# Three steps by seven block products, placed late, in the attention groups of a two-layer decoder trunk

## The chip, the cores and the metric

The kernel runs on one core of a Trainium2 chip. The metric is the device time of one execution in microseconds (us); the times named are medians of three runs. Lower is better. Engine names are those of the profile: PE is the matrix engine, PEld its weight loads, DVE the vector engine, ACT the scalar engine, SP the engine whose queue issues the weight transfers.

## The reference

A two-layer decoder trunk on a sequence of 256 tokens, width 2048, all in float32. Layer 0 mixes tokens by causal trailing means, layer 1 by differential attention; each is followed by a SwiGLU block. The change concerns layer 1:

```python
hn = rmsnorm(h, norm_mix[1])
qkv = hn @ w_qkv                       # 2048 x 6144: q, k, v
s = q k^T / sqrt(128) + ALiBi bias, causal;  p = softmax(s), for each of 8 heads twice
a = p[:, :, 0] - lam * p[:, :, 1]
o = rmsnorm(a @ v) * subln_g * (1 - lambda_init)
h = h + o @ w_o                        # 2048 x 2048
h = h + (silu(hn2 @ wg) * (hn2 @ wu)) @ wd     # 5632 wide, both layers
```

## The kernel before, in words

Every large product is made in **groups**. A group is the 256-token activation times 1024 columns of weights, summed over the whole contraction of 2048 in eight **steps** of 256 each. A step takes one transfer of 1 MB from the SP queue (`raw`, three buffers, L109): four blocks B12, B11, B22, B21 of 128 x 512 weights. Float32 accuracy comes from splitting each operand into a high half and a low half: ACT casts `raw` to `whi` (L115), DVE subtracts to get `wlo` (L116); these two have three buffers each. Each block product is then three PE matmuls of 512 columns: high by high, high by low, low by high (L178 to L180).

A **plain** step has eight block products, 24 matmuls, into PSUM banks 4 to 7. A step **by seven** uses a Strassen-Winograd form: seven block products, 21 matmuls, of which some take sums of blocks. For these DVE makes the sums `tsum` (L121, L123, L124; one buffer), ACT their high half `thi` (L130), DVE their low half `tlo` (L131). Only three of the four raw blocks have to be split then (`whi`, `wlo` of 1536 columns in place of 2048). Its products go to all eight banks; banks 0 to 3 are used by no plain step. When a group ends, `combined` (L195) adds the banks up.

Banks 0 to 3 also serve as scratch (`aux`) for everything between the groups: transposes, attention scores, the products with v. So a step by seven cannot begin before the scratch work that was put into the group's early steps has let go of these banks.

The activations are prepared once: `pair` (L245) transposes 256 of the contraction and splits it, for a step by seven with eight slots (four blocks and four sums of them), otherwise with four. `products` (L163) can run a plain step from either layout.

The groups in layer 1 are: four for q and k (L574; each followed by two attention heads, `head` L544, whose work falls into the next group's early steps), two for v (L593; each followed by four heads' output work), two for the output projection (L612). Then come the groups of the SwiGLU block. The lists `SEVEN...` name the step numbers done by seven: 2, 4 and 6 in the SwiGLU groups, 4 and 6 in those of attention, in the order 0 to 7.

The tiles `tsum`, `thi`, `tlo` and the four sums `c` lie in the pool of the stage: `qk_sums` while q and k are made, `out` for v and the output. Pool `attn_tmp` holds a head's working tiles. The order of each engine's instructions is set at compile time by a list scheduler from the program's order and a model of readiness; each engine then runs its own list in order, and semaphores make it wait.

## Time and profile before

| | before |
|---|---|
| median of 3 runs (lowest to highest) | 1843.76 us (1843.35 to 1843.92) |
| profiled execution, its own time | 1843.5 us |
| its span, first to last instruction | 1841.7 us |
| mean granted PE clock | 0.999 |
| PE busy | 1825.5 us, 8201 matmuls |
| DVE busy | 1615.7 us |
| ACT busy | 1043.0 us |
| HBM traffic | 353.36 MB read, 193 GB/s |
| transfers of 1 MB for q and k, v, output | 32, 16, 16 |

Busy times are unions of an engine's instructions. A matmul's duration in the profile is longer than the distance from one to the next, because they are pipelined; the distance is read from start times. A wait is put down to the engine that released it.

### The profile page before, as it was taken

What the parts mean: (1) busy time and instruction counts of PE and PEld (TensorE: products, weight loads), DVE (VectorE), ACT (ScalarE), POOL (GpSimd) and SP (SyncE); (2) the same over time, 40 slices, a digit from 0 to 9 for tenths busy, and PEclk for the clock granted to TensorE, in tenths of its full rate; (3) what the DMA queues carried; (4) which work ended last, traced back from release to release, by engine and by line L of the source; (5) the groups of instructions that cost most, each with busy time, mean ns of one, the idle gap of its engine ahead of it and who ended that gap; (6) DMA issues with size and microseconds to landing.
All of it is one profiled execution on the core that took longest, in us unless ns stands there. A gap on an engine that the chain in (4) does not pass through costs nothing.

```text
span 1841.7 us, 20907 instructions
## 1 busy us (share of the span) xinstructions
PE 1825.5 (99%) x8201; PEld 1493.0 (81%) x8201; DVE 1615.7 (88%) x1676; ACT 1043.0 (57%) x1010; POOL 0.7 (0%) x6
## 2 busy tenths in 40 slices
PE   9999999999999999999999999999999999999998
PEld 6788888888888888888888888788888888888886
DVE  6989998898989899988878779998989899998986
ACT  6655545556554556665566666555555555545553
POOL 0000000000000000000000000000000000000000
PEclk9999999999999999999999999999999999999999
DMA  7555555555555555554554454555555555565552
GB/s 274 183 205 183 198 210 192 211 195 196 202 197 204 201 188 183 206 183 168 176 175 169 168 183 175 209 201 187 204 203 206 191 197 186 207 225 206 202 189 112
DMA packets 50642, 356.80 MB, mean 194 GB/s; under 512 B 6000, under 2 KB 6128, under 8 KB 8048
## 3 DMA queue, kind: packets, MB, share of 16 engines
q1 hardware_dynamic: 49824, 353.85, 54.5%
q10 hardware_dynamic: 720, 1.62, 0.2%
q8 instruction: 64, 1.05, 0.2%
q14 instruction: 34, 0.28, 0.0%
HBM read 353.36 MB, written 2.10 MB: 193 GB/s over the span
## 4 chain that ended last, share of the span: by engine, by line
PE 95%; DVE 2%; ACT 1%; issue 1%; DMA 1%; SPq 0%; DVEq 0%; ACTq 0%
PE b L180 90%; PE b L250 2%; DVE wlo L116 1%; PE b L554 1%; PE b L345 1%; DMA x_tok<-x_n 1%; PE b L584 0%; PE b L342 0%; DMA raw<-w_gu 0%; DVE tlo L131 0%; ACT whi L115 0%; PE b L600 0%; DVE tsum L121 0%; PE b L598 0%; PE b L599 0%
## 5 line engine op out<-in xcount | busy, mean ns | idle before, releaser
L115 ACT CAST whi<-raw 128x1536 fp32r<-128x1536 f32 (+1 forms) x330 | 583.9, 1770 | 572.7 <-PE b L180 486.6
L180 PE MATMUL b<-whi,xp 128*128 128x512 f32 x2814 | 905.9, 392 | 0.8 <-DVE c L203 0.7
L116 DVE TENSOR_TENSOR wlo<-raw,whi 128x1536 fp32r<-128x1536 f32 (+1 forms) x330 | 695.5, 2108 | 178.8 <-ACT whi L115 178.6
L180 PEld LDWEIGHTS b<-whi,xp 128*128 128x128 f32 x2814 | 526.3, 188 | 109.7 <-DVE c L203 1.1
L180 PE MATMUL b<-wlo,xp 128*128 128x512 f32 x1407 | 550.0, 391 | 1.7 <-DVE wlo L116 1.7
L180 PE MATMUL b<-whi,h 128*128 128x512 f32 x1108 | 354.5, 390 | 0.0
L180 PEld LDWEIGHTS b<-wlo,xp 128*128 128x128 f32 x1407 | 264.3, 188 | 55.2 <-DVE wlo L116 1.9
L131 DVE TENSOR_TENSOR tlo<-tsum,thi 128x2048 fp32r<-128x2048 f32 x111 | 253.6, 2284 | 8.0 <-ACT thi L130 8.0
L180 PEld LDWEIGHTS b<-whi,h 128*128 128x128 f32 x1108 | 207.4, 188 | 43.2
L130 ACT CAST thi<-tsum 128x2048 fp32r<-128x2048 f32 x111 | 211.9, 1909 | 16.7 <-DVE tsum L124 16.6
L180 PE MATMUL b<-wlo,h 128*128 128x512 f32 x554 | 215.8, 390 | 0.0
L180 PE MATMUL b<-thi,xp 128*128 128x512 f32 x616 | 214.7, 390 | 0.0
L121 DVE TENSOR_TENSOR tsum<-raw 128x1024 f32<-128x1024 f32 x111 | 135.4, 1220 | 2.1 <-DMA raw<-w_v 0.5
L180 PEld LDWEIGHTS b<-thi,xp 128*128 128x128 f32 x616 | 115.4, 188 | 24.4 <-ACT thi L130 0.9
L180 PEld LDWEIGHTS b<-wlo,h 128*128 128x128 f32 x554 | 104.0, 188 | 21.3
L180 PE MATMUL b<-tlo,xp 128*128 128x512 f32 x308 | 121.1, 393 | 0.0
L180 PE MATMUL b<-thi,h 128*128 128x512 f32 x240 | 83.7, 389 | 0.0
L124 DVE TENSOR_TENSOR tsum<-tsum,raw 128x512 f32<-128x512 f32 x111 | 76.4, 688 | 2.2
L123 DVE TENSOR_TENSOR tsum<-tsum,raw 128x512 f32<-128x512 f32 x111 | 76.0, 684 | 0.7
L180 PEld LDWEIGHTS b<-tlo,xp 128*128 128x128 f32 x308 | 57.8, 188 | 16.3 <-DVE tlo L131 4.5
L180 PE MATMUL b<-whi,oT 128*128 128x512 f32 x216 | 69.1, 393 | 0.0
L180 PEld LDWEIGHTS b<-thi,h 128*128 128x128 f32 x240 | 45.1, 188 | 9.2
(147 smaller groups left out, 1196.4 us busy)
## 6 DMA issues: line engine op xcount, KB each, us to landing
raw<-w_gu SPq DMA_DIRECT2D x176, 1024.0 KB, 4.8
raw<-w_down SPq DMA_DIRECT2D x88, 1024.0 KB, 4.8
raw<-w_qk SPq DMA_DIRECT2D x32, 1024.0 KB, 4.8
raw<-w_v SPq DMA_DIRECT2D x16, 1024.0 KB, 4.9
raw<-w_o SPq DMA_DIRECT2D x16, 1024.0 KB, 4.8
raw<-pool_w SPq DMA_DIRECT2D x2, 1024.0 KB, 14.0
x_tok<-x_n SPq DMA_DIRECT2D x2, 768.0 KB, 8.8
w<-pool_w SPq DMA_DIRECT2D x2, 512.0 KB, 6.3
```

Of the source, the lines that this page charges most:

```text
L115: nc.scalar.copy(hi[:, lo_block:], raw[:, lo_block:])
L116: nc.vector.tensor_tensor(lo[:, lo_block:], raw[:, lo_block:], f32(hi[:, lo_block:]), ALU.subtract)
L121: nc.vector.tensor_tensor(t[:, T1:T3 + 1], raw[:, B11:B22 + 1], raw[:, B12:B12 + 1].broadcast_to([P, 2, 512]), ALU.add)
L123: nc.vector.tensor_tensor(t[:, T2], t[:, T1], raw[:, B22], ALU.add)
L124: nc.vector.tensor_tensor(t[:, T4], t[:, T2], raw[:, B21], ALU.add)
L130: nc.scalar.copy(hi, t)
L131: nc.vector.tensor_tensor(lo, t, f32(hi), ALU.subtract)
L180: nc.tensor.matmul(ps[b], x, y[:, block], start=first, stop=(left[b] == 0))
L250: nc.tensor.transpose(ps[:, i, 1 - t if seven else t], src(i, t), ident)
L345: nc.tensor.matmul(yp[g][t], u, v[:, at], start=(at == 0 and j == 0), stop=(at == 3 and j == 2))
L554: nc.tensor.matmul(sc[:, :nk], qk[:, 0, c, qb * P:(qb + 1) * P], qk[:, 1, c, :nk], start=True, stop=True)
```

## The change

Step 2 joins the steps by seven in the four groups of q and k, the two of v and the first of the output; the second output group keeps 4 and 6. In the seven changed groups the steps run in the order 0, 1, 3, 5, 4, 2, 6, 7, so that the three by seven stand fifth, sixth and seventh. `thi` and `tlo` get two buffers there. To make room in SBUF, the head's `bias` tile goes from two buffers to one and `qk` from three to two. The activation tiles of step 2 (`xp2`, `oT2`) are prepared with eight slots.

```diff
-SEVEN_QKV = (4, 6)
-SEVEN_O = (4, 6)
+SEVEN_QKV = (2, 4, 6)
+SEVEN_O = (2, 4, 6)
+
+LATE = (0, 1, 3, 5, 4, 2, 6, 7)
...
-    def sum_halves(pool, t):
-        hi = pool.tile([P, 4, 512], F32R, name="thi")
-        lo = pool.tile([P, 4, 512], F32R, name="tlo")
+    def sum_halves(pool, t, bufs):
+        hi = pool.tile([P, 4, 512], F32R, name="thi", bufs=bufs)
+        lo = pool.tile([P, 4, 512], F32R, name="tlo", bufs=bufs)
...
-    def group(steps, pool, by_bank=0):
+    def group(steps, pool, by_bank=0, bufs=1):
...
-                w.append(sum_halves(pool, t))
+                w.append(sum_halves(pool, t, bufs))
...
-            bias = at.tile([P, 2 * P], F32, name="bias")
+            bias = at.tile([P, 2 * P], F32, name="bias", bufs=1)
...
-            cs = combined(group([(xp[p], p in SEVEN_QKV, w_qk[g, p]) for p in range(NP)], hq), hq)
+            cs = combined(group([(xp[p], p in SEVEN_QKV, w_qk[g, p]) for p in LATE], hq, bufs=2), hq)
...
-                qk = at.tile([P, 2, 2, S], F32, name="qk", bufs=3)
+                qk = at.tile([P, 2, 2, S], F32, name="qk")
...
-            cs = scaled(combined(group([(xp[p], p in SEVEN_QKV, w_v[g, p]) for p in range(NP)], op_), op_), (r_col, r_col))
+            cs = scaled(combined(group([(xp[p], p in SEVEN_QKV, w_v[g, p]) for p in LATE], op_, bufs=2), op_), (r_col, r_col))
...
-        for g in range(2):
-            cs = combined(group([(oT[p], p in SEVEN_O, w_o[g, p]) for p in range(NP)], op_), op_)
+        for g, (by_seven, order) in enumerate(((SEVEN_O, LATE), (SEVEN_O[1:], range(NP)))):
+            cs = combined(group([(oT[p], p in by_seven, w_o[g, p]) for p in order], op_, bufs=2), op_)
```

## The prediction

> **What bounds the kernel now.** I read the page's first part, then the grouped instructions by shape, the windows, the waits, and the timeline of single groups.

> ```profile
> span 1841.7 us, 20907 instructions
> PE 1825.5 (99%) x8201; PEld 1493.0 (81%) x8201; DVE 1615.7 (88%) x1676; ACT 1043.0 (57%) x1010; POOL 0.7 (0%) x6
> ```
> ```profile
> core 0: us, PE busy (x) PEld busy (x) DVE busy (x) ACT busy (x) POOL busy (x), PEclk, DMA share, GB/s
> 853.70:901.50 47.80, 47.80 (x226) 38.92 (x225) 38.94 (x62) 28.89 (x42) 0.00 (x0) 1.00 0.51 176
> 239.00:282.00 43.00, 43.00 (x191) 35.63 (x190) 39.06 (x34) 21.52 (x14) 0.00 (x0) 1.00 0.58 213
> 820.20:835.70 15.50, 15.50 (x70) 12.83 (x69) 8.48 (x5) 8.28 (x7) 0.00 (x0) 1.00 0.58 204
> ```
> ```profile
> PE b L180 <- DVE wlo L116: 1.7, 1, 1.7
> PE b L325 <- DVE xt L328: 2.0, 2, 1.7
> ```

> The windows are one period of the q and k groups with its two heads, a stretch of the SwiGLU block, and the second half of a q and k group. PE is busy in all of each; DVE has idle time, 8.86 us of 47.8 in the q and k period (47.80 - 38.94). The last two rows head PE's list of waits in the whole span: 1.7 and 2.0 us in all. So PE bounds, and what PE doesn't have to do comes off the time as long as DVE and ACT still feed it. DVE is the next engine, at 88%.

> How far apart are matmuls? A plain step of the first q and k group:

> ```profile
> 778.51 0.61 PE L180 MATMUL b<-whi,xp 128*128 128x512 f32 x2
> ...
> 783.95 0.61 PE L180 MATMUL b<-whi,xp 128*128 128x512 f32 x2
> ```

> The pattern (two, then one with `wlo`) repeats eight times between these two starts: 24 matmuls in 5.44 us, 0.2267 us each. A plain step costs PE 24 x 0.2267 = 5.44 us, one by seven 21 x 0.2267 = 4.76 us.

> **The change part by part.** *PE.* Seven groups lose three matmuls each: 21 x 0.2267 = **-4.76 us**. Nothing is added: `pair` makes four transposes in either layout, `combined` is needed already, and the banks are the same. Four plain steps still stand ahead of the first step by seven, so the scratch banks are asked back as late as now. [...]

> *DVE and ACT.*

> ```profile
> L116 DVE TENSOR_TENSOR wlo<-raw,whi 128x2048 fp32r<-128x2048 f32 x219 | 501.1, 2289 | 162.8 <-ACT whi L115 162.8
> L131 DVE TENSOR_TENSOR tlo<-tsum,thi 128x2048 fp32r<-128x2048 f32 x111 | 253.6, 2284 | 8.0 <-ACT thi L130 8.0
> L130 ACT CAST thi<-tsum 128x2048 fp32r<-128x2048 f32 x111 | 211.9, 1909 | 16.7 <-DVE tsum L124 16.6
> L116 DVE TENSOR_TENSOR wlo<-raw,whi 128x1536 fp32r<-128x1536 f32 x111 | 194.4, 1752 | 16.0 <-ACT whi L115 15.7
> L121 DVE TENSOR_TENSOR tsum<-raw 128x1024 f32<-128x1024 f32 x111 | 135.4, 1220 | 2.1 <-DMA raw<-w_v 0.5
> L124 DVE TENSOR_TENSOR tsum<-tsum,raw 128x512 f32<-128x512 f32 x111 | 76.4, 688 | 2.2
> L123 DVE TENSOR_TENSOR tsum<-tsum,raw 128x512 f32<-128x512 f32 x111 | 76.0, 684 | 0.7
> L268 DVE TENSOR_TENSOR xp<-e,xp 128x1024 fp32r<-128x1024 f32 x8 | 9.7, 1218 | 0.7 <-ACT xp L267 0.7
> L546 DVE TENSOR_SCALAR bias<-dist_sb 128x256 f32<-128x256 f32 x8 | 2.3, 284 | 0.0
> ```

> A step by seven costs DVE 1.220 + 0.684 + 0.688 = 2.59 us of sums, 1.75 of `wlo`, 2.28 of `tlo`, 6.63 in all; a plain one 2.29. So each changed group gives DVE 4.34 us more, seven of them 30.4 us, and ACT at most one `thi`, 1.91. Two tiles with eight slots (`xp2`, `oT2`) add a pass like the 1.22 us one, to a DVE that is idle 9% there. DVE comes to about 1648 us, 90% of the span. This lies beside PE and costs nothing as long as each half is there when PE wants it; a q and k period would hold 38.94 + 4.34 = 43.28 us of DVE in 47.80 - 0.68 = 47.12, which leaves 3.84 us idle.

> The question is therefore order in time. Three steps by seven in a row use 3 x 4.76 = 14.28 us of PE and 3 x 6.63 = 19.9 us of DVE: DVE must be ahead. And `tsum` has one buffer: sums, `thi` and `tlo` of one step (2.59 + 1.91 + 2.28 = 6.78 us) must end before the next sums start. PE wants the first `tlo` seven matmuls into a step, 1.6 us. I walk through it three times.

> *A q and k group with heads beside it* (three of these).

> ```profile
> 817.91 2.28 DVE L116 TENSOR_TENSOR wlo<-raw,whi 128x2048 fp32r<-128x2048 f32 x1
> 822.84 1.76 DVE L116 TENSOR_TENSOR wlo<-raw,whi 128x1536 fp32r<-128x1536 f32 x1 [2.64 <-ACT whi L115]
> 827.39 2.29 DVE L116 TENSOR_TENSOR wlo<-raw,whi 128x2048 fp32r<-128x2048 f32 x1 [2.80 <-ACT whi L115]
> 829.60 2.28 DVE L131 TENSOR_TENSOR tlo<-tsum,thi 128x2048 fp32r<-128x2048 f32 x1
> ```
> ```profile
> 822.48 0.39 PE L180 MATMUL b<-thi,xp 128*128 128x512 f32 x1
> ```
> ```profile
> 827.26 1.90 ACT L130 CAST thi<-tsum 128x2048 fp32r<-128x2048 f32 x1
> ```

> The first `thi` is the seventh matmul of the first step by seven, which so began at 821.12. At 817.91 the heads are done on DVE and the next sums are already made; from there DVE waits 2.64 and 2.80 us, for `whi` buffers that PE frees. After the change: `wlo` to 819.7, `tlo` of the second to 822.5 (its `thi` has its own buffer), sums of the third to 825.1, its `wlo` to 826.9. Its `thi` can begin once PE has left the first step's, at 825.9, or behind the cast of the plain step's `whi`, 827.4; `tlo` ends between 830.2 and 831.9. PE starts that step at 821.12 + 2 x 4.76 = 830.64 and wants `tlo` at 832.2. In time, by 0.3 us at worst. Loss 0 (at worst, one place later in DVE's order, about 1 us a group).

> *The first q and k group.*

> ```profile
> 768.38 2.28 DVE L131 TENSOR_TENSOR tlo<-tsum,thi 128x2048 fp32r<-128x2048 f32 x1
> ...
> 774.06 1.22 DVE L121 TENSOR_TENSOR tsum<-raw 128x1024 f32<-128x1024 f32 x1
> ```
> ```profile
> 774.66 0.39 PE L180 MATMUL b<-thi,xp 128*128 128x512 f32 x1
> ```

> Here the first step by seven begins at 773.3, and the second sums only at 774.06, though `tsum` is free when the first `tlo` ends at 770.66. If they are made then, two chains of 6.78 end at 784.2, or 785.4 with an operand's 1.22 us pass between; wanted at 773.3 + 9.52 + 1.6 = 784.4. Loss 0 to 1.0.

> *The first v group.*

> ```profile
> 957.53 0.48 DVE L570 SCALAR_TENSOR_TENSOR a_sb<-p_sb,l_inv 128x256 f32<-128x256 f32 x1
> 957.94 1.22 DVE L121 TENSOR_TENSOR tsum<-raw 128x1024 f32<-128x1024 f32 x1
> ...
> 963.62 2.28 DVE L131 TENSOR_TENSOR tlo<-tsum,thi 128x2048 fp32r<-128x2048 f32 x1
> ```
> ```profile
> 966.10 0.39 PE L180 MATMUL b<-thi,xp 128*128 128x512 f32 x1
> 966.33 0.39 PE L180 MATMUL b<-tlo,xp 128*128 128x512 f32 x1
> ```
> ```profile
> 937.58 0.33 SPq L109 DMA_DIRECT2D raw<-w_v  x1
> ```

> This is the tight place. The sums' transfer was issued at 937.58, yet they begin at 957.94, right behind the last head's last operation: the v sums are in pool `out`, which comes after the heads' pools. `tlo` ends at 965.9 and is read at 966.33, 0.4 us later. The step began at 964.74. Three chains of 6.78 from 957.94, with `wlo` set into the casts, end at 978.3 to 979.1; in the plain order PE would want the third `tlo` at 964.74 + 9.52 + 1.6 = 975.9. That is 3.1 us late at worst. PE need not stand, though; its order is fitted to this:

> ```profile
> 740.63 0.84 PE L180 MATMUL b<-thi,h 128*128 128x512 f32 x3
> ...
> 742.90 0.39 PE L180 MATMUL b<-tlo,h 128*128 128x512 f32 x1
> ```

> There three `thi` products of three banks run first and `tlo` is first read ten matmuls later; in the same way thirteen matmuls of a step (2.95 us) can precede its `tlo`, and after them the plain step 7, whose halves are ready by 976.8 (974.5, where the third sums end, and one `wlo`). Loss 0 to 3.1; nearest is the swap row, so I take 0.5 us for this and the first group together.

> *The rest.* The second v group and the output group start their sums some 20 us ahead: loss 0. Step 5 moves forward by two places, to fourth: its operand must be there three plain steps (16.3 us) after a group's start.

> ```profile
> 749.47 0.39 PE L180 MATMUL b<-whi,xp 128*128 128x512 f32 x1
> ...
> 757.44 0.48 DVE L243 SCALAR_TENSOR_TENSOR xp<-b,gain_sb,xp 128x256 fp32r<-128x256 f32 x1
> ```
> ```profile
> 1036.70 0.58 PE L180 MATMUL b<-whi,oT 128*128 128x512 f32 x1
> ...
> 1051.22 0.48 DVE L243 SCALAR_TENSOR_TENSOR oT<-b,small,oT 128x256 fp32r<-128x256 f32 x1
> ```

> `xp5` is ready at 757.9, wanted at 765.8. `oT5` follows at about 1052.6, wanted at 1036.7 + 16.3 and the scratch matmuls between: 1053 or later. The 48 transfers stay as many and in step. `bias` with one buffer makes a head's 0.28 us wait until the same engine has read the one before: 0 to 0.28 a head, taken as 0 since scores come later. Two `qk` buffers still hold a group's two heads.

> Sum: -4.76 + 0.5 = -4.3 us on the profiled execution's 1843.5, 1839.2. The median of the runs lies 0.26 above that execution, so **1839.5 us**.

> **The rivals.** *Part of it is eaten (within 0.2%).* The loss reaches more than 1.07 us: 3.1 in the first v group, 1.0 in the first, or a place in the order lost in three groups. For it: the row with 0.4 us of room, and DVE at 92% of a q and k period. If DVE can fill no more than the 90.8% of the SwiGLU window (39.06 of 43.00), a period takes 43.28 / 0.908 = 47.66 in place of 47.12, four times 0.54: about 1841.6. Against it: that window isn't DVE's limit, as PE is full there.

> *Slower: DVE's in-order waits stay.* If the 8.86 us that DVE waits in a q and k period cannot be filled, because the instruction at the head of its list waits for a `whi` and holds those behind it, the period becomes 43.28 + 8.86 = 52.1 us, +4.3 in four groups, with -0.7 in three: +15.1, 1858.9. It decides from 4.5 us of idle per period upward (3.84 + 0.68). The waits of 2.64 and 2.80 show that it happens now. [...] Against: the waits are for buffers that PE frees, and DVE has spare work exactly there now.

> *A matmul is worth less than its distance.* If the 0.2267 us were set by the weights' arrival and not by PE, removing matmuls would bring less: 1843.8 where it brings nothing. Against: the distance is the same in a whole plain step, and a `wlo` is made every few us, not with each matmul. [...]

> **How the numbers follow.** This kernel tells a difference of about 0.2% (3.7 us) from no change. Forecast: 0.60, its own range 1838.4 to 1840.1. Eaten in part: 0.27. Worth less: 0.05. Slower by over 0.2%: 0.08. So faster 0.60, same 0.32, slower 0.08. For 8 in 10 the range runs from 1838.4 (all of 4.76 and 0.6 of spread between runs) to 1843.4, where the eaten case ends.

> **What would show it.** Right: 21 matmuls less, DVE near 1648 us, the q and k period near 47.1 us with PE full, thirteen or so matmuls before the first `tlo` in the v group. Wrong: PE waiting for `tlo` or `wlo` by over 1 us in the first v group or in each q and k group, or a period above 47.8 us.

## The result, and the profile after

| | before | after |
|---|---|---|
| median (lowest to highest), 6 runs each | 1843.63 us (1843.25 to 1843.92) | 1853.12 us (1851.93 to 1856.51) |
| ratio | | 1.0055, 95% interval 1.0044 to 1.0065 |
| profiled execution, its span | 1843.5, 1841.7 us | 1856.51, 1854.7 us |
| mean granted PE clock of that execution | 0.999 | 0.995 |

The changed kernel is slower by 9.5 us; 1839.5 was forecast. Its runs also lie 4.6 us apart, those of before 0.7 us. The profiled execution is the slowest of the six, so its losses in the trace are larger than those of the median. In all listings of the changed kernel line numbers are two higher than before (L182 is the matmul, L118 `wlo`, L133 `tlo`, L132 `thi`).

The page of after, its span and first part:

```profile
span 1854.7 us, 20907 instructions
...
PE 1830.9 (99%) x8180; PEld 1491.7 (80%) x8180; DVE 1647.7 (89%) x1708; ACT 1052.5 (57%) x1019; POOL 0.7 (0%) x6
```

There are 21 matmuls fewer in the records (8180 for 8201), and yet PE is busy 5.4 us longer (1830.9 for 1825.5). DVE's 1647.7 us is the 1648 of the forecast. So the work is what was reckoned, and something makes both PE's waits and its matmuls longer. First the waits of PE in the whole span, largest first (total, times, longest):

```profile
PE b L182 <- ACT thi L132: 2.8, 2, 1.4
PE b L182 <- DVE tlo L133: 2.6, 2, 1.3
PE b L182 <- DVE wlo L118: 2.4, 2, 1.7
...
PE b L252 <- ACT o_n L610: 1.9, 1, 1.9
```

Before, PE waited nowhere for `thi` or `tlo`, once 1.7 us for `wlo`, and 0.2 for `o_n`. Where they are, in PE's timeline (start, busy time, the wait in brackets):

```profile
791.34 1.19 PE L182 MATMUL b<-thi,xp 128*128 128x512 f32 x4 [1.40 <-ACT thi L132]
793.80 0.80 PE L182 MATMUL b<-tlo,xp 128*128 128x512 f32 x1 [1.27 <-DVE tlo L133]
794.39 0.63 PE L182 MATMUL b<-thi,xp 128*128 128x512 f32 x1
794.82 0.63 PE L182 MATMUL b<-tlo,xp 128*128 128x512 f32 x1
...
986.16 1.20 PE L182 MATMUL b<-thi,xp 128*128 128x512 f32 x4 [1.41 <-ACT thi L132]
988.68 0.80 PE L182 MATMUL b<-tlo,xp 128*128 128x512 f32 x1 [1.32 <-DVE tlo L133]
...
1040.42 0.50 PE L182 MATMUL b<-wlo,xp 128*128 128x512 f32 x1 [0.70 <-DVE wlo L118]
...
1068.18 0.91 PE L252 MATMUL b<-ident,o_n 128*128 128x128 f32 x4 [1.94 <-ACT o_n L610]
```

791 and 794 are the third step by seven of the first q and k group, 986 and 989 that of the first v group; 1040 lies in the second v group, 1068 at the first output group. And behind the waits each matmul starts 0.43 us after the one before (794.39, 794.82), not 0.227. The windows show why, in the column behind POOL, the granted clock:

```profile
787.00:790.00 3.00, 2.94 (x13) 2.09 (x12) 3.00 (x3) 2.54 (x2) 0.00 (x0) 1.00 0.27 38
792.00:795.00 3.00, 1.73 (x6) 1.10 (x5) 1.75 (x1) 0.00 (x0) 0.00 (x0) 0.72 1.01 421
986.00:989.00 3.00, 1.52 (x5) 1.00 (x6) 2.62 (x2) 0.11 (x1) 0.00 (x0) 0.81 0.96 347
989.00:992.00 3.00, 3.00 (x8) 2.33 (x8) 1.98 (x3) 0.36 (x1) 0.00 (x0) 0.50 1.01 404
1070.00:1073.00 3.00, 3.00 (x10) 1.93 (x9) 2.69 (x2) 2.22 (x8) 0.00 (x0) 0.50 0.83 270
868.60:915.70 47.10, 47.10 (x220) 37.63 (x219) 42.90 (x67) 29.39 (x42) 0.00 (x0) 1.00 0.50 174
```

The trace's clock record has the clock at one half from 793.32 for 3.41 us, from 987.88 for 6.83 us and from 1069.80 for 3.41 us. In the kernel before it is full from 4.91 to 1837.87 us. The last row is a stretch of q and k with its heads: there PE is full at full clock. Its length is chosen and is not the period; from the first transposes of one q and k group's result to those of the next, the three periods took 47.49, 47.70 and 47.30 us, where they had taken 47.83, 47.81 and 47.79.

What DVE does ahead of the two waits at 791 and 794, in its timeline (the first row begins the second step's sums):

```profile
773.00 1.22 DVE L123 TENSOR_TENSOR tsum<-raw 128x1024 f32<-128x1024 f32 x1
...
782.27 2.28 DVE L133 TENSOR_TENSOR tlo<-tsum,thi 128x2048 fp32r<-128x2048 f32 x1
784.59 1.22 DVE L123 TENSOR_TENSOR tsum<-raw 128x1024 f32<-128x1024 f32 x1
785.85 0.69 DVE L125 TENSOR_TENSOR tsum<-tsum,raw 128x512 f32<-128x512 f32 x1
786.46 2.29 DVE L118 TENSOR_TENSOR wlo<-raw,whi 128x2048 fp32r<-128x2048 f32 x1
788.66 0.68 DVE L126 TENSOR_TENSOR tsum<-tsum,raw 128x512 f32<-128x512 f32 x1
789.26 2.28 DVE L118 TENSOR_TENSOR wlo<-raw,whi 128x2048 fp32r<-128x2048 f32 x1
791.47 2.28 DVE L133 TENSOR_TENSOR tlo<-tsum,thi 128x2048 fp32r<-128x2048 f32 x1
```

The third step's sums begin the moment the second step's `tlo` has ended (784.55), and between them and their own `tlo` stand two `wlo` of 2048 columns, the splits of whole plain steps: the first two of the *next* group. The first of them holds up the sums by 2.2 us; the second runs while ACT makes `thi` (789.38 to 791.29) and adds little. The same picture stands in the first v group, from 979.42 to 986.34.

For the profiled execution (span +13.0 us): -4.76 for the matmuls, +7.8 of new waits (1.40 + 1.27 + 1.41 + 1.32 + 0.70 + 1.94 - 0.2), and for 13.65 us at half clock at most half of that, 6.8. That makes 9.9. The three periods of the other q and k groups shrank by 0.94 us in all, where nine matmuls are 2.04: 1.1 more, from matmuls that stand wider apart (more on them at the end of the experiments). Some 2.0 us stay unplaced.

### The profile page after: what moved, and what is told of

It reads as the page before. It is cut to its first block, busy times and chain, and to the rows that moved or that the text cites. A ratio compares the mean times of both kernels' runs of the same rounds, so it can differ in the third digit from the quotient of the medians.

```text
span 1854.7 us, 20907 instructions
## 1 busy us (share of the span) xinstructions
PE 1830.9 (99%) x8180; PEld 1491.7 (80%) x8180; DVE 1647.7 (89%) x1708; ACT 1052.5 (57%) x1019; POOL 0.7 (0%) x6
## 3 DMA queue, kind: packets, MB, share of 16 engines
q8 instruction: 64, 1.05, 0.2%
## 4 chain that ended last, share of the span: by engine, by line
PE 92%; DVE 4%; ACT 1%; DMA 1%; issue 1%; SPq 0%; DVEq 0%; ACTq 0%
PE b L182 87%; PE b L252 2%; DVE wlo L118 1%; ACT whi L117 1%; PE b L556 1%; DVE tlo L133 1%; PE b L347 1%; DMA x_tok<-x_n 0%; PE b L344 0%; PE b L586 0%; DMA raw<-w_down 0%; DMA raw<-w_gu 0%; DMA raw<-w_v 0%; DVE tsum L123 0%; PE b L602 0%
## 5 line engine op out<-in xcount | busy, mean ns | idle before, releaser
L182 PE MATMUL b<-whi,xp 128*128 128x512 f32 x2754 | 890.7, 393 | 1.0 <-DVE c L205 0.9
L118 DVE TENSOR_TENSOR wlo<-raw,whi 128x1536 fp32r<-128x1536 f32 (+1 forms) x330 | 692.2, 2098 | 153.9 <-ACT whi L117 153.3
L182 PEld LDWEIGHTS b<-whi,xp 128*128 128x128 f32 x2754 | 515.4, 188 | 108.4 <-DVE c L205 1.3
L182 PE MATMUL b<-wlo,xp 128*128 128x512 f32 x1377 | 539.2, 392 | 2.4 <-DVE wlo L118 2.4
L182 PE MATMUL b<-whi,h 128*128 128x512 f32 x1108 | 354.3, 391 | 0.0
L182 PEld LDWEIGHTS b<-wlo,xp 128*128 128x128 f32 x1377 | 259.0, 188 | 55.3 <-DVE wlo L118 3.0
L133 DVE TENSOR_TENSOR tlo<-tsum,thi 128x2048 fp32r<-128x2048 f32 x118 | 269.7, 2286 | 9.0 <-ACT thi L132 8.8
L182 PEld LDWEIGHTS b<-whi,h 128*128 128x128 f32 x1108 | 207.5, 188 | 43.2
L182 PE MATMUL b<-thi,xp 128*128 128x512 f32 x664 | 233.7, 394 | 2.8 <-ACT thi L132 2.8
L132 ACT CAST thi<-tsum 128x2048 fp32r<-128x2048 f32 x118 | 225.1, 1908 | 11.8 <-DVE tsum L126 11.3
L182 PE MATMUL b<-wlo,h 128*128 128x512 f32 x554 | 215.9, 390 | 0.0
L182 PEld LDWEIGHTS b<-thi,xp 128*128 128x128 f32 x664 | 125.2, 189 | 30.8 <-ACT thi L132 5.3
L123 DVE TENSOR_TENSOR tsum<-raw 128x1024 f32<-128x1024 f32 x118 | 144.0, 1220 | 2.1 <-DMA raw<-w_down 0.5
L182 PE MATMUL b<-tlo,xp 128*128 128x512 f32 x332 | 133.2, 401 | 2.6 <-DVE tlo L133 2.6
L182 PEld LDWEIGHTS b<-wlo,h 128*128 128x128 f32 x554 | 104.0, 188 | 21.2
L182 PE MATMUL b<-thi,h 128*128 128x512 f32 x240 | 83.8, 390 | 0.0
L126 DVE TENSOR_TENSOR tsum<-tsum,raw 128x512 f32<-128x512 f32 x118 | 81.2, 689 | 2.4
L125 DVE TENSOR_TENSOR tsum<-tsum,raw 128x512 f32<-128x512 f32 x118 | 80.8, 685 | 0.8
L182 PEld LDWEIGHTS b<-tlo,xp 128*128 128x128 f32 x332 | 63.4, 191 | 21.6 <-DVE tlo L133 8.5
L182 PE MATMUL b<-whi,oT 128*128 128x512 f32 x206 | 67.3, 397 | 0.0
L207 ACT COPY c<-b 128x512 f32<-128x512 f32 x41 | 24.1, 588 | 53.8 <-PE b L182 53.8
```

The source lines that it names most:

```text
L118: nc.vector.tensor_tensor(lo[:, lo_block:], raw[:, lo_block:], f32(hi[:, lo_block:]), ALU.subtract)
L123: nc.vector.tensor_tensor(t[:, T1:T3 + 1], raw[:, B11:B22 + 1], raw[:, B12:B12 + 1].broadcast_to([P, 2, 512]), ALU.add)
L125: nc.vector.tensor_tensor(t[:, T2], t[:, T1], raw[:, B22], ALU.add)
L126: nc.vector.tensor_tensor(t[:, T4], t[:, T2], raw[:, B21], ALU.add)
L132: nc.scalar.copy(hi, t)
L133: nc.vector.tensor_tensor(lo, t, f32(hi), ALU.subtract)
```

## The experiments

Theory A: the loss sits in the two groups whose sums can't start early, the first q and k group and the first v group; the third chain of sums, `thi` and `tlo` is late there. Rival B: DVE has too much work in all changed groups. All but the waits study were timed beside the kernel before on the same chip (1843.75 to 1843.86 in the four sessions). "After" in an edit is the changed kernel.

| kernel | median, us | ratio to before, 95% interval |
|---|---|---|
| first groups undone | 1842.18 | 0.9992 (0.9983 to 1.0001) |
| plain step between | 1849.98 | 1.0035 (1.0023 to 1.0048) |
| zero matmuls | 1854.67 | 1.0058 (1.0045 to 1.0071) |
| buffers only | 1843.85 | 1.0002 (0.9993 to 1.0011) |
| first v group undone | 1846.75 | 1.0017 (1.0008 to 1.0026) |
| third sums reused | 1841.17 | 0.9987 (0.9979 to 0.9996) |
| q and k groups 2 to 4 alone | 1843.18 | 0.9997 (0.9988 to 1.0006) |
| one pool, first q and k undone | **1841.66** | 0.9987 (0.9978 to 0.9996) |
| after, one pool | 1845.12 | 1.0007 (0.9998 to 1.0016) |
| before, one pool | 1843.77 | 1.0000 (0.9991 to 1.0009) |
| one pool, spread | 1847.25 | 1.0019 (1.0010 to 1.0028) |
| next group's splits bare | 1847.71 | 1.0020 (1.0011 to 1.0029) |
| one pool, two `tsum` | 1842.37 | 0.9994 (0.9985 to 1.0003) |
| the best one, two `tsum` | 1842.19 | 0.9992 (0.9983 to 1.0001) |

### Where: the first groups undone, and the first v group alone

First groups undone (the q and k line; the v line in the same way):

```diff
-            cs = combined(group([(xp[p], p in SEVEN_QKV, w_qk[g, p]) for p in LATE], hq, bufs=2), hq)
+            cs = combined(group([(xp[p], p in (SEVEN_QKV if g else SEVEN_QKV[1:]), w_qk[g, p]) for p in (LATE if g else range(NP))], hq, bufs=2), hq)
```

> The first q and k group and the first v group go back to steps 4 and 6 by seven in the order 0 to 7 (buffers as changed); the other five groups stay changed. Theory A (the third step by seven is late only where a stage's sums start late, in these two groups; PE waits there and its clock is then halved for windows of 3.41 us): the waits of 1.40 + 1.27 and 1.41 + 1.32 us and the 10.2 us at half clock go, two groups take 0.68 us more each: 1853.1 - 5.4 - 5.1 + 1.4 = about 1844. Theory B (DVE is too full everywhere, so the lost time follows the total of DVE work, of which 8.7 of 30.4 us goes): about 1853.1 - 0.29 x 9.5 = 1850.

Measured 1842.18: below even A's figure, 10.9 us less than after, with 15 of the 21 matmuls still saved. The waits at the second v group and the first output group are gone too, though these groups are as in the changed kernel.

The v line alone undone:

> Only the first v group goes back to two steps by seven in the order 0 to 7; the first q and k group keeps three. Theory A (the loss sits in the two groups whose sums start late, and what stands still behind the first v group follows from it): the first q and k group still costs its waits of 1.4 and 1.3 us and some half clock, the waits in the second v group (0.70) and the first output group (1.94) are gone: 1842.2 + 3 to 4 = 1845 to 1846.5. Theory B (more work on DVE in each changed group, wherever it stands): one changed group less of seven, so about a seventh of the loss of 14 us is gone: 1851. If the waits behind v come from those groups themselves, 1848 to 1849.

Measured 1846.75, 0.25 above A's range. The two waits of 1.4 and 1.3 us in the first q and k group stay, with 3.41 us of half clock behind them (mean granted clock 0.998; 0.995 in after); nothing is left of the waits at 986, 989, 1040 and 1068. So the third step by seven costs 4.6 us net in the first q and k group (1846.75 - 1842.18), and 6.4 in the first v group with the waits that come behind it (1853.12 - 1846.75). B falls: five groups with the full DVE load lose nothing against before.

### Which: the halves of the third step

Third sums reused: in these two groups the third step takes the second's `thi` and `tlo`. This leaves the third step's own sums out of the result; PE's work stays the same.

```diff
+            kept = made[1] if seven and reuse and len(made) == 2 else None
-            t = sums(pool, raw) if seven else None
+            t = sums(pool, raw) if seven and kept is None else None
...
-                w.append(sum_halves(pool, t, bufs))
+                w.append(kept or sum_halves(pool, t, bufs))
```

> In the first q and k group and the first v group the third step by seven makes no sums of its own and takes those of the second step (so the sums of blocks are left out of the computation there); the matmuls, 21 fewer than before, and the transfers stay. DVE does 9.7 us less in all. Theory A (PE waits because the chain of sums, thi and tlo of the third step ends late): both waits and the half clock behind them go, and the groups bring their matmuls: 1842.2 - 1.4 = 1840.8, within 1839.5 to 1842. Theory B (DVE's total is too long): 9.7 us of 1648 less change little: 1850 or above.

Measured 1841.17, 11.95 us less than after, with the same matmuls and transfers. Windows over the places where PE had waited (PE is the first busy column):

```profile
777.00:822.00 45.00, 45.00 (x211) 36.23 (x210) 41.09 (x65) 27.81 (x38) 0.00 (x0) 1.00 0.55 193
...
964.00:1008.00 44.00, 44.00 (x199) 35.52 (x199) 38.41 (x49) 31.39 (x49) 0.00 (x0) 1.00 0.56 198
1059.00:1103.00 44.00, 44.00 (x206) 35.77 (x205) 39.49 (x49) 29.49 (x40) 0.00 (x0) 1.00 0.52 179
```

PE is full and the clock whole in all three: the loss is that chain.

### Why late: the next group's splits

The first two steps of the second q and k group and of the second v group make no `wlo` and use `whi` in its place, which leaves the low half of these weights out:

```diff
+        if one:
+            nc.scalar.copy(hi, raw)
+            return hi, hi
...
-            cs = combined(group([(xp[p], p in SEVEN_QKV, w_qk[g, p]) for p in LATE], hq, bufs=2), hq)
+            cs = combined(group([(xp[p], p in SEVEN_QKV, w_qk[g, p]) for p in LATE], hq, bufs=2, bare=2 if g == 1 else 0), hq)
```

> The changed kernel, in which the first two (plain) steps of the second q and k group and of the second v group make no low half of their weights and take the high half in its place (left out of the computation there); their matmuls and casts stay. It takes four instructions of 2.29 us off DVE, the ones that stand between the third step's sums and its low half in the groups before. Theory A1 (the next group's splits, put into the third step's chain, make it late): that chain is 2.4 to 4.4 us shorter in both groups, the waits of 1.4 and 1.3 us go but for some tenths, the half clock with them: 1841 to 1843. Theory A2 (the chain is late already when its sums begin): the waits shrink by less than half, 1848 or more.

Measured 1847.71, just below the 1848 of A2 and far from A1's 1841 to 1843. Its waits:

```profile
PE b L187 <- DVE wlo L121: 2.3, 2, 1.7
PE b L257 <- ACT o_n L615: 1.9, 1, 1.9
...
PE b L187 <- DVE tlo L136: 1.3, 2, 0.7
```

In the two groups the wait for `thi` is gone, that for `tlo` halved, and the half clock behind both gone: 5.4 us of waits have become 1.3. In the waits that is A1. The waits farther on stay in full (0.7 for a `wlo` in the second v group; 1.9 for `o_n`, with 3.41 us of half clock; mean granted clock 0.997), and they keep the time high. The third chain of the first q and k group, in its DVE timeline:

```profile
785.32 1.23 DVE L126 TENSOR_TENSOR tsum<-raw 128x1024 f32<-128x1024 f32 x1
786.58 0.69 DVE L128 TENSOR_TENSOR tsum<-tsum,raw 128x512 f32<-128x512 f32 x1
787.30 0.69 DVE L129 TENSOR_TENSOR tsum<-tsum,raw 128x512 f32<-128x512 f32 x1
789.97 2.29 DVE L136 TENSOR_TENSOR tlo<-tsum,thi 128x2048 fp32r<-128x2048 f32 x1 [1.98 <-ACT thi L135]
```

From 785.32 to 792.26 it takes 6.94 us, the 6.78 of the forecast; with the two `wlo` in it, 784.59 to 793.75, it took 9.16. So the splits are 2.2 us of the lateness, and a wait of 0.7 a group is there without them, as the sums begin late: A1 in the main, not alone.

### Why late: the pool, and the buffer

One pool: the pool `qk_sums` stays open to the end of the attention, and v and output groups take it in place of `out`.

```diff
-with tc.tile_pool(name="attn", ...) as ap_, ExitStack() as heads:
-    hq = heads.enter_context(tc.tile_pool(name="qk_sums", ...))
+with tc.tile_pool(name="attn", ...) as ap_, tc.tile_pool(name="qk_sums", ...) as hq, ExitStack() as heads:
...
-cs = scaled(combined(group([... w_v[g, p]) for p in LATE], op_, bufs=2), op_), (r_col, r_col))
+cs = scaled(combined(group([... w_v[g, p]) for p in LATE], hq, bufs=2), hq), (r_col, r_col))
```

After with it, before with it, and after with it and the first q and k group undone:

> The changed kernel with the one pool for sums and nothing else. Theory A: the loss at the first v group and what followed it goes, that of the first q and k group stays (4.6 us by the two kernels with and without it, 1846.75 - 1842.18): 1841.5 + 4.6 = 1846. If the pool isn't the cause: 1853.

> The kernel before with the one pool for sums and nothing else; what the pool is worth by itself. PE doesn't wait in the v group of the kernel before, so 1843.8, no difference; anything over 0.5 us would have to be taken off the gain of the other two.

> The first q and k group back to two steps by seven; all v and output groups make their sums, thi, tlo and c in the pool of the q and k stage, which now stays open to the end of the attention, so that the first v group's sums need not wait for the heads' pools to be given back. 18 matmuls fewer than before. Theory A with this cause (the late pool makes the chain late): sums of the first v group start before 957.9, PE doesn't wait there, 1842.18 - 0.68 = 1841.5 (1840.5 to 1842.3). If the order on DVE alone makes the chain late, whatever the pool: waits for thi and tlo of over 1 us as in the changed kernel, 1845 or more.

Measured 1845.12, 1843.77 and 1841.66: the first theory's figures within 0.9 us. The pool by itself is worth nothing; with the third step in the v group it is worth 8 us (1853.12 - 1845.12). In the third kernel, the fastest but for the one with reused sums, the chain of the first v group is spread among the heads' work (DVE):

```profile
940.91 1.22 DVE L123 TENSOR_TENSOR tsum<-raw 128x1024 f32<-128x1024 f32 x1
...
952.71 1.22 DVE L123 TENSOR_TENSOR tsum<-raw 128x1024 f32<-128x1024 f32 x1
...
964.55 1.23 DVE L123 TENSOR_TENSOR tsum<-raw 128x1024 f32<-128x1024 f32 x1
...
972.56 2.29 DVE L133 TENSOR_TENSOR tlo<-tsum,thi 128x2048 fp32r<-128x2048 f32 x1
```

The first sums begin at 940.91, where they had begun at 957.94 before the change; the third `tlo` ends at 974.85.

Then the buffer, in after with one pool, and in the best kernel: two for `tsum`, one for `tlo`.

```diff
-        t = pool.tile([P, 4, 512], F32, name="tsum")
+        t = pool.tile([P, 4, 512], F32, name="tsum", bufs=bufs)
...
-        lo = pool.tile([P, 4, 512], F32R, name="tlo", bufs=bufs)
+        lo = pool.tile([P, 4, 512], F32R, name="tlo", bufs=1)
```

> The kernel with the one pool and all seven groups by seven late (1845.12), with two buffers for the sums and one for their low half, in place of one and two. If the third step's sums of the first q and k group are held up because the second step's low half must be done with the sums' only buffer (they begin at 784.59, 0.04 us behind it): they begin some 4 us earlier, PE's two waits there go, 1841 to 1842. If what else stands on DVE's list sets it, or the one buffer for the low half brings a wait of its own: 1844.5 or more.

> The best kernel so far (one pool, the first q and k group with two steps by seven, 1841.66) with the same buffers. PE waits nowhere in those groups, so there is nothing to gain: 1841.7, within 0.5. If one buffer for the low half is too few where three steps by seven follow each other, waits appear and it is above 1842.5.

Measured 1842.37 and 1842.19. In the first kernel the waits for `thi` and `tlo` in the first q and k group are gone, 2.75 us less than with one `tsum` (1845.12). Its DVE timeline:

```profile
777.80 1.22 DVE L123 TENSOR_TENSOR tsum<-raw 128x1024 f32<-128x1024 f32 x1
...
784.62 2.29 DVE L133 TENSOR_TENSOR tlo<-tsum,thi 128x2048 fp32r<-128x2048 f32 x1
...
787.29 2.29 DVE L118 TENSOR_TENSOR wlo<-raw,whi 128x2048 fp32r<-128x2048 f32 x1 [0.19 <-ACT whi L117]
789.50 2.29 DVE L133 TENSOR_TENSOR tlo<-tsum,thi 128x2048 fp32r<-128x2048 f32 x1
```

The third sums now begin ahead of the second `tlo`, not behind it, 3.5 us after the second step's first sum (774.33; in after 11.6, 773.00 to 784.59); the third `tlo` ends 17.5 us after it (20.8 in after), with a `wlo` of the next group still in front. So the second buffer was put at the wrong tile: `tlo` got it, `tsum` held the chain. In the best kernel the exchange costs 0.5 us, on the edge of what can be told.

### Other orders: two misses and a half

A plain step between (order 0, 1, 3, 5, 4, 2, 7, 6 in the two groups):

> As changed, but in the first q and k group and the first v group the plain step 7 stands between the second and the third step by seven (order 0, 1, 3, 5, 4, 2, 7, 6). No work is taken away. Theory A: PE wants the third tlo 5.4 us later, its waits and the half clock of these two groups go: 1853.1 - 10.5 = about 1843. Theory B (DVE's total is the limit): no gain, 1853.

Measured 1849.98. Most of the waits for the halves go, but a group that ends by seven brings another (its PE waits):

```profile
PE b L183 <- DVE c L206: 5.4, 3, 3.6
...
PE b L183 <- DVE tlo L134: 0.7, 1, 0.7
```

The next group's plain products go to banks that `combined` has still to read, and PE stands 3.6 us at 986. Neither theory had that.

One pool, spread (order 0, 1, 3, 2, 5, 4, 6, 7 in the first q and k group):

> The one pool, all seven groups with three steps by seven, and in the first q and k group the order 0, 1, 3, 2, 5, 4, 6, 7, in which a plain step stands between the first step by seven and the other two: 5.44 us more for the chain of the second and third, but the first is wanted 5.4 us earlier. If the chain's length against the time that PE leaves for it decides: PE waits less than 1 us there, 1841.5 - 0.68 = 1840.8. If the first sums can't be made earlier (they begin at about 763.5 in the kernel before), PE waits for the first step: 1843 to 1846.

Measured 1847.25, a miss: PE doesn't wait for the first step, as the second case had it, but still for the last (`thi` 2.1 us, `tlo` 1.3 us, half clock for 6.83 us; mean granted clock 0.997). The second step's `tlo` still ends at 785.12, no earlier than in the order LATE (784.55), and the third's sums follow it, at 785.15: in this list one `tsum` orders the chain wherever the step stands.

Zero matmuls: six matmuls with zero weights, twice, into the third step in the two groups, 24 in all, 5.44 us.

```diff
+                if fill and last_seven and i == 2:
+                    for _ in range(fill):
+                        nc.tensor.matmul(ps[M2], zero, w[0][0][:, B21], start=False, stop=False)
```

> As changed, with 12 matmuls by a zero matrix added to PE in each of the same two groups, placed by the scheduler ahead of the third step's thi and tlo: 2.7 us of work where PE waited 2.7 us. The result is the same. If the halved clock follows from PE's idling (theory A), the waits become work, the clock stays full there and the time falls by about 5.1 us, to 1848. If the clock falls for another reason, or the wait follows PE's work, the time rises by up to 5.4 us, to 1853 to 1858.

Measured 1854.67, not lower. The waits for `thi` and the half clock in both groups went, the two for `tlo` (1.3 us each) stayed, and so did the wait for `o_n` with its 3.41 us of half clock (mean granted clock 0.997; 0.995 in after). The 5.44 us of matmuls cost more than they saved: the half clock went with the waits for `thi`, but it wasn't bought off this way.

### What costs nothing, and what a group is worth

Buffers alone, in the kernel before (two each for `thi` and `tlo`, one `bias`, two `qk`):

> The kernel before with the changed buffers alone: two for thi and tlo in the attention groups, one for bias, two for qk; steps 4 and 6 by seven in the order 0 to 7. Theory A and B: 1843.6, as before. Rival (the head's tighter buffers delay the scratch work): 1845 to 1850.

Measured 1843.85: nothing.

The second to fourth q and k groups alone:

> Only the second to fourth q and k groups take three steps by seven; the first of them, both v groups and both output groups stand as before: 9 matmuls fewer. If each group brings its 0.68 us: 1843.77 - 2.04 = 1841.7. If these groups bring only half of it, since products of different steps stand further apart when they are interleaved, 1842.8; and if the second v group and the first output group bring what is missing in the kernel with five changed groups (1842.18), this one is above that by 0.7 to 1.4.

Measured 1843.18, 0.59 us below before where 9 matmuls are 2.04; with this interval the gain isn't told from none. PE waits in none of these groups, so the matmuls themselves stand wider. Counted from the start times, what the distances between block products have over 0.227 us sums to 0.93 us in the second q and k period (856 to 904 us) of the kernel before and to 1.38 in this one; over the four periods it grows by 1.05, of the 1.45 that are missing. Most of it is in distances of 0.29 to 0.36 us: in that period two `whi` products that follow each other stand so far apart 5 times, before twice. What makes them wide stays open.

## Why the prediction was wrong, point by point

*Matmuls and engines.* 21 fewer and 1647.7 us of DVE are right. That a matmul's distance is what it is worth was right where it was asked last, and too high in total: with no wait left (third sums reused) the change brings 2.6 us of 4.76. The 227 ns are PE's own: in the kernel of bursts and waits (below) one row has 110 matmuls while DVE, ACT and DMA do nothing (the window from 144 has 3 us of it), (25.21 - 0.39) / 109 = 0.228 us each.

*The q and k groups with heads: loss 0.* Right as to waits (PE full, 47.10 of 47.10), and as to the margin: in the second group the third `tlo` ended at 837.01 and was read at 837.35. (In its sum the second `tlo` ends at 822.5; its own terms, 817.91 + 1.75 + 2.28, give 821.9, to the safe side.) Not seen were the wider distances: the periods came to 47.3 to 47.7 us, not to the 47.12 of the sum.

*The first q and k group: 0 to 1.0.* This step failed. It let the second chain begin where the first `tlo` had ended (770.66) and took 6.78 us for a chain. The second began at 773.00, behind another pass and a `tlo` that ended at 771.88, and took 11.55 (to 784.55); the third took 9.16 (784.59 to 793.75). So the end, put at 784.2, came 9.5 us later: 2.3 from the start, 4.8 and 2.4 from the chains' lengths. PE covered most of it with products that don't need the third `tlo`, and waited 2.7. Into the second chain went two `wlo` of 1536 and one of 2048 columns. ACT's list did its part:

```profile
778.12 1.91 ACT L117 CAST whi<-raw 128x2048 fp32r<-128x2048 f32 x1 [2.59 <-PE b L182]
779.93 1.92 ACT L132 CAST thi<-tsum 128x2048 fp32r<-128x2048 f32 x1
```

The second `thi` stood behind a cast that had waited 2.59 us for a `whi` buffer that PE had to free. Its sums had ended at 778.83 and it began at 779.93, so 1.1 us of the chain is this. The price of the group: 2.7 us of waits and, in that execution, 3.41 us at half clock, 4.6 us by the two medians.

*The first v group: 0 to 3.1, taken as 0.5.* The place of the lateness was named, but two things were wrong. The chains were again too short: the end was put at 978.3 to 979.1 and was 988.6. Of this, 3.9 us are a later start (961.82 for 957.94) and cost nothing by themselves, as PE's first `thi` product came just as much later (969.98 for 966.10); the rest is the chains, 7.2, 10.4 and 9.2 us for three of 6.78. And the cover was used up: PE did draw products of the plain step 7 forward (from 981.42 to 984.37 it runs `whi` and `wlo` products alone), and then waited 1.41 and 1.32 us. For this group and the first together 0.5 us was put into the sum; by the medians they cost 11.0 (4.6 + 6.4, net of the matmuls that they save and with the waits behind the v group).

*The second v group and the output group: 0.* Wrong: 0.70 and 1.94 us. Both are gone when the first v group goes back to two steps by seven, or reuses the sums. They aren't its lost time carried on, though: with the next group's splits bare its waits are down to 0.7 us and these two stay as they were. At the output group ACT's list has `o_n` behind a cast that waits for PE:

```profile
1066.28 1.47 ACT L117 CAST whi<-raw 128x1536 fp32r<-128x1536 f32 x1 [1.47 <-PE b L182]
1067.65 0.83 ACT L610 ACTIVATE o_n<-b,rs_r 128x256 f32<-128x256 f32 x2
```

The same order stands in the kernel with bare splits. Why the compiled order is another one in the kernels without these waits stays open.

*Buffers and `bias`: 0.* Right. But the second `tlo` buffer was taken as help; the single `tsum`, named in the working as the tile that orders the chain, was not priced against a second buffer.

*The rivals.* "Part of it is eaten" had the right two places and capped their price at 4.1 us. "Slower: DVE's in-order waits stay" had the right mechanism and the wrong place: it looked for idle time in the q and k periods, where PE never waited. Neither they nor the sum had the clock, which was put at nothing: behind the waits of 2.7 us in the two groups came 3.41 and 6.83 us at half clock, up to 1.7 and 3.4 us more.

## What to carry to other kernels

When three or more dependent steps are pushed together, price the chain with what the compiled order of each engine can put in between, above all the splits of the *next* group, and ask which single buffer hands the chain on; the second buffer belongs there. Look where a stage's tiles come into being: sums in a pool that opens only when the stage before has closed began 14 us later here than in one that stays open (957.94 and 943.51, the kernel before and the same with one pool). And look at the granted clock behind PE's waits: here 2.7 us of waits in each of two groups were followed by 3.41 and 6.83 us at half clock, up to 1.7 and 3.4 us more.

## What the runs showed of the hardware

The clock's drop was not expected. Its cost differs from run to run: the six runs of the changed kernel have a mean granted clock of 0.998 (1851.93, 1852.31 and 1852.52 us), 0.997 (1853.72), 0.996 (1854.76) and 0.995 (1856.51), time following clock. Waits of several lengths, single and in pairs, were measured by themselves:

```diff
+    def wait(b, hops):
+        nc.scalar.copy(got, b[:, 0:256])
+        last = got
+        for k in range(hops):
+            nc.vector.tensor_copy(hop[k % 2], last)
+            last = hop[k % 2]
+        nc.vector.tensor_scalar(rhs[:, 0:1], last[:, 0:1], 0.0, None, ALU.mult)
```

> Not the decoder: bursts of 110 to 119 matmuls of 128x512, between which PE waits for a chain of one ACT copy and 0 to 10 DVE copies that starts from its own result, and pairs of waits with 5, 10 or 20 matmuls between. The output is not computed. If the clock is halved by the length of a single wait, the records show it full after waits up to some length between 1.66 and 1.94 us and halved after all longer ones. If it goes by the share of idle time in fixed stretches of 3.41 us, one and the same wait halves it at one place and not at another, and two waits of 1.3 us within some 2.5 us halve it more often than one of 1.7 us.

Rows of its PE timeline, and windows (granted clock behind POOL, as above):

```profile
114.31 4.29 PE L84 MATMUL b<-rhs,wgt 128*128 128x512 f32 x12 [1.80 <-DVE rhs L93]
...
143.29 25.21 PE L84 MATMUL b<-rhs,wgt 128*128 128x512 f32 x110 [2.13 <-DVE rhs L93]
...
376.34 4.18 PE L84 MATMUL b<-rhs,wgt 128*128 128x512 f32 x9 [1.47 <-DVE rhs L93]
...
882.97 7.32 PE L84 MATMUL b<-rhs,wgt 128*128 128x512 f32 x31 [1.47 <-DVE rhs L93]
```
```profile
114.00:117.00 3.00, 2.69 (x9) 2.20 (x10) 0.15 (x1) 0.00 (x0) 0.00 (x0) 0.78 0.00 0
...
144.00:147.00 3.00, 3.00 (x14) 2.46 (x14) 0.00 (x0) 0.00 (x0) 0.00 (x0) 1.00 0.00 0
...
375.50:378.50 3.00, 2.16 (x5) 1.82 (x6) 0.55 (x3) 0.00 (x0) 0.00 (x0) 0.50 0.00 0
...
884.00:887.00 3.00, 3.00 (x15) 2.47 (x14) 0.00 (x0) 0.00 (x0) 0.00 (x0) 1.00 0.00 0
```

Behind a wait of 1.80 us the clock was halved (0.78 over the window from 114), behind one of 2.13 it was not (1.00 from 144); behind a pair of 1.47 us it was at 376 (0.50) and was not at 883 (1.00). So it isn't the wait's length alone: behind the same pair the clock was halved at one place and not at another, as the second theory of the expectation has it. By the 0.78 the clock fell at 115.68; by the windows around 375 it fell between 375.0 and 375.5, and 76 times 3.413 us after 115.68 is 375.09. From these numbers comes an estimate for the pairs: with steps of 3.413 us on from 115.68, the first wait at 376 and the beginning of the second lie in one stretch (371.68 to 375.09), and at 883 a boundary (880.27) parts them.

The records of full clock begin 4.84 us after the first instruction in the changed kernel and 4.91 in the kernel before. If the grid lies elsewhere against the program from run to run and the waits are alike, which no second trace of the changed kernel shows, this would fit the spread of its times.
